# A fused trunk layer on TensorE: the first two products of four projection units are moved between the io projection's second and third product, with 83 working slots instead of 77

## The chip, the cores and the metric

The kernel runs on one core of one Trainium2 chip. The metric is the time of one execution on the device in microseconds (us); lower is better. The kernel before was timed in three runs. One further execution was recorded by the profiler, and all rows of the trace come from that one.

## The reference

The reference computes one layer of a streaming-encoder trunk on a sequence of 2048 rows of width 1024, in fp32:

```python
x_n = rmsnorm(x)
z   = x_n @ W_in          # columns: pool | q | forget | input v | output gate | branch gates
a   = pool_mixer(u)       # trailing means over 2/4/8/16 rows, minus the token, 4 groups of 128
f   = lb + (1 - lb) * sigmoid(zf)
k, q = 1 - f, silu(zq)
S_t = diag(f_t) S_{t-1} + k_t v_t^T          # 4 heads of 128, chunks of 64 rows
o_t = S_t^T q_t ;  o = rmsnorm(o) * silu(zo)
x   = x + (ga * (a @ W_pa) + gb * (o @ W_pb)) @ W_o      # ga, gb = sigmoid(x_n @ W_g + bias)
x   = x + (silu(gate) * val) @ W_down        # val, gate: conv3(rmsnorm(x) @ W_up), d_ff = 2816
out = rmsnorm(x)
```

## The kernel before, in words

**Tiling.** The sequence is cut into four blocks of 512 rows. Two blocks form a pass: the pass `b0 = 0` takes blocks 0 and 1, the pass `b0 = 2` takes blocks 2 and 3, and each runs `mixer` and then `ffn`. Every large product is computed by Strassen-Winograd on 2 x 2 quarters: seven quarter products, P1 to P7, in place of eight, with sums of quarters before and after them. An fp32 operand is split into a high and a low part of type fp32r, and each quarter product is made of three matmuls (high by high, high by low, low by high).

**The forms of x.** Each of the seven products takes its own form of the transposed input (`FORM`): P1 takes B11 and P2 takes B21. Both belong to the pass's first block (in the trace `x_f0h` to `x_f7l`) and are ready before the second block's. P6, P5, P7 and P4 take T2, T1, T3 and T4, sums that contain the second block, and P3 takes B22, the second block itself. The second block is transposed by 32 matmuls of 128 x 128 on TensorE (L646), which write PSUM; VectorE scales and adds them (`x_t`, L703), and each form is then split by a cast on ScalarE (L597) and a subtraction on VectorE (L598).

**The io projection.** `proj_io` (L1105 to L1156) computes v and the output gate z. Its seven products come in the order `IO_ORDER`, P1, P2, P6, P5, P7, P4, P3, and each has 4 x 4 x 3 = 48 matmuls of 128 x 512. P1 leaves `e1` (a copy on ScalarE), P2 gives the first half of v, P6 gives `u2` = e1 - Z (L1133), P7 gives `u3` = Z - e1 (L1135) and the second half of z, P4 the first half of z, and P3 the second half of v. P6, P7 and P4 accumulate in the same four PSUM banks Z, in turn: P4 can overwrite a bank only after `u3` has read it. The product of z with its sigmoid is on GpSimd for one half and on VectorE for the other (L1124).

**The units.** The other columns of W_in are 14 units, listed in `PROJ`: four of kind fq (forget gate and q of a head), two of kind u (the pool branch) and eight of kind g (branch gates). A unit is seven products of 12 matmuls each, in the order `ORDER`, P1, P6, P5, P7, P2, P4, P3. P1 writes the bank X, which ScalarE copies to `e1` (L1018, the names end in `_e`). P2 accumulates onto X, and so must wait for that copy. After P2, a unit's first output is final in X: for fq it is the forget gate (sigmoid at L1189, then L808 on VectorE), for g it is a branch gate (sigmoid at L1234, then a store at L791).

**The weights.** `Stream` holds two planned lists. The raw list is tiles of 256 KB, loaded by SyncE's DMA queue in list order (L182) into `N_RAW = 8` buffers; a buffer is loaded again when its last user has been issued. The operand list is high and low parts, made by a cast on ScalarE (L205) and a subtraction on VectorE (L206) in `N_OPS = 6` buffers. Where a product wants a sum of quarters, the sum is made first, by `plan_io` (L338) for the io projection and by `weights_of_unit` (L397) for a unit, on GpSimd or VectorE. In the pass `b0 = 0` these sums are stored to DRAM (L310), and the pass `b0 = 2` loads them instead of adding again (`sums_of_unit`).

**The order.** The program is written as a loop of products, with side work (forms, the HGRN recurrence, pooling, gates) in tasks that are stepped every 6 matmuls. A list scheduler then sets the order of the instructions of each engine; on the chip each engine takes its list strictly in that order. Working tiles (`e1`, `u2`, gates, q, f) come from a pool of `N_SLOTS = 77` slots of 2112 bytes per partition, and PSUM has 8 banks. When the io projection is over, `prep.append(Task(prepare()))` starts the preparation of later weights by adding DMAs.

Of the kernel before, what the change touches and what calls it, by code (L numbers as in the profile page):

```python
# [49 lines left out]
ORDER = ("P1", "P6", "P5", "P7", "P2", "P4", "P3")  # L50
IO_ORDER = ("P1", "P2", "P6", "P5", "P7", "P4", "P3")
# [5 lines left out]

M_ORDER = (0, 4, 1, 5, 2, 6, 3, 7)

N_SLOTS = 77  # L60
# [18 lines left out]
def tile_trunk(  # L79
# [238 lines left out]
    def plan_io(b0):  # L318
        for p in IO_ORDER:
# [25 lines left out]
    def plan_unit(key, src, kind, i, order, b0):  # L345
        mv, mg = proj_tiles(kind, i)
        if b0:
            unit = sums_of_unit(src, mv, mg, lambda p: lambda: kept["in", (kind, i), SUM_OF[p]])
        else:
            unit = weights_of_unit(src[mv], src[mg], (kind, i))  # L350
        for p in order:
            fn, raws = unit[p]()
            stream.op(key, fn, raws)

    def plan_mixer(b0):
        plan_io(b0)
        for kind, i in PROJ:
            if (kind, i) == ("u", 0):
                plan_one("pw", pool_wt)
            plan_unit("in", w_in_t, kind, i, ORDER, b0)  # L360
# [25 lines left out]
    def weights_of_unit(src_v, src_g, unit):  # L386
# [15 lines left out]
        def plan(p):  # L402
            if p == "P5":
                return (lambda nm: tmp["s1"]), []
            rs = [raw(i) for i in {"P1": (0,), "P2": (1,), "P4": (3,), "P6": (0, 2, 3),
# [700 lines left out]
    def proj_io(b0, forms, late, vd, zd):  # L1106
# [35 lines left out]
        for p in IO_ORDER:  # L1142
# [14 lines left out]

    def mixer(b0, forms, late):
# [5 lines left out]
        proj_io(b0, forms, late, vd, zd)  # L1164
        if b0 == 0:
            prep.append(Task(prepare()))

# [94 lines left out]
        for n, (kind, i) in enumerate(PROJ):  # L1262
            if (kind, i) == ("u", 0):
                held["w"] = stream.get("pw")
            u = Unit(f"{kind[0]}r{b0}_{i}", "in", emits[kind](i))
            for p in ORDER:
                u.multiply(p, forms, late)
                u.after(p)
                if n == len(PROJ) - 1 and p == "P1":
                    mtask = Task(pa_task())  # L1270
# [318 lines left out]
```

## Time and profile before

| what | value |
|---|---|
| median of 3 runs | 2622.06 us (2621.85 to 2622.27) |
| span of the profiled execution | 2614.3 us |
| TensorE busy in it | 2533.7 us (97%) |
| TensorE not busy | 80.6 us |
| VectorE / ScalarE / GpSimd busy | 1967.4 / 1168.9 / 909.3 us |
| mean granted TensorE clock | 0.989 of full speed |

The span runs from the first to the last instruction. The median of the runs is 7.8 us longer, which lies outside the span. A row of the timeline has the start, the time, the engine, the line, the operation with its output and inputs, the count of instructions, and in brackets the idle time just before it and what ended that. The granted clock is the share of full TensorE speed that the chip allowed in a stretch.

### The profile page before, as it was taken

To read this page: it belongs to the slowest core of one execution; us is meant where nothing else is said; L and a number is where in the kernel's file an instruction comes from. 1 tells how busy PE (TensorE), PEld (TensorE's weight loads), DVE (VectorE), ACT (ScalarE), POOL (GpSimd) and SP (SyncE) were. 2 spreads that over 40 slices of the span, in tenths; PEclk is the share of its full clock that TensorE was granted. 3 is DMA by queue.
4 is the path that set the end of the run, shared out by engine and by line. 5 is a ranking of instruction groups with operands and counts; after the bars stand their busy time and mean duration, and the time that the engine had idled before them with its cause. 6 is when DMAs were issued, how large, how long until landed. Compare 5 with 4: busy or idle time off the path is not lost. (4 is left out here: it accounts for less than half of the span.)

```text
span 2614.3 us, 35569 instructions
## 1 busy us (share of the span) xinstructions
PE 2533.7 (97%) x11464; PEld 2064.8 (79%) x11464; DVE 1967.4 (75%) x3390; ACT 1168.9 (45%) x2204; POOL 909.3 (35%) x1253
## 2 busy tenths in 40 slices
PE   7899999989999999999999999999999999999998
PEld 6788888767778888878878788887787888887887
DVE  7898779358799877876476787774778987787845
ACT  5333434224555544555364344442345554445633
POOL 5544343062444343362141111200623433335402
PEclk9999999999999999999999999999999999999999
DMA  6887868888778897587365344346452445545943
GB/s 221 274 213 211 224 189 242 268 275 214 198 188 241 243 240 198 165 305 255 108 195 157 101 135 121 116 145 218 142 173 84 151 150 148 141 141 185 377 142 105
DMA packets 254059, 496.90 MB, mean 190 GB/s; under 512 B 26736, under 2 KB 43248, under 8 KB 253552
## 3 DMA queue, kind: packets, MB, share of 16 engines
q1 hardware_dynamic: 187968, 319.89, 38.9%
q0 software_dynamic: 41504, 110.64, 16.6%
q10 hardware_dynamic: 24400, 64.08, 7.1%
q8 instruction: 91, 1.49, 0.2%
q14 instruction: 96, 0.79, 0.1%
HBM read 384.94 MB, written 187.17 MB: 219 GB/s over the span
## 5 line engine op out<-in xcount | busy, mean ns | idle before, releaser
L205 ACT CAST ops<-raw 128x512 fp32r<-128x512 f32 x732 | 451.6, 620 | 780.1 <-PE dn_P L145 141.1
L206 DVE TENSOR_TENSOR ops<-raw,ops 128x512 fp32r<-128x512 f32 x732 | 564.1, 775 | 214.2 <-ACT ops L205 208.7
L1381 DVE SCALAR_TENSOR_TENSOR e<-h,cols,e 128x512 f32<-128x512 f32 x176 | 142.4, 813 | 29.9 <-ACT e L1379 26.1
L1379 ACT ACTIVATE e<-h,cols 128x512 f32<-128x512 f32 x176 | 142.6, 814 | 24.2 <-DVE h L984 16.9
L1384 DVE SCALAR_TENSOR_TENSOR e<-h,cols,e 128x512 f32<-128x512 f32 x176 | 133.9, 769 | 3.0
L796 POOL DMA_DIRECT2D g_P<-dg_P x154 | 83.7, 545 | 107.6 <-PE dn_P L145 70.0
L1090 POOL TENSOR_TENSOR gf_P<-e,e 128x512 f32<-128x512 f32 x44 | 67.8, 1542 | 153.1 <-DVE e L1390 97.8
L1090 POOL TENSOR_TENSOR gf_P<-gf_P,e 128x512 f32<-128x512 f32 x44 | 60.1, 1366 | 68.5 <-DVE e L1390 68.1
L1374 POOL COPY h<-h 128x2 f32<-128x2 f32 x88 | 40.7, 482 | 113.9 <-DVE h L982 112.0
L1301 POOL TENSOR_TENSOR ya<-ya,gl 128x512 f32<-128x512 f32 x32 | 45.8, 1460 | 98.4 <-issue 49.1
L1376 POOL COPY hist<-h 128x2 f32<-128x2 f32 x88 | 35.3, 401 | 127.3 <-DVE h L984 125.6
L1234 ACT ACTIVATE gt<-gt,cols 128x512 f32<-128x512 f32 x48 | 34.8, 724 | 90.5 <-DVE gt L984 71.1
L1388 ACT ACTIVATE e<-e 128x512 f32<-128x512 f32 x88 | 55.5, 631 | 37.9 <-DVE e L1384 37.4
L984 DVE TENSOR_TENSOR h<-up_u,up_V 128x512 f32<-128x512 f32 x88 | 60.2, 684 | 15.2 <-PE up_V L145 14.8
L1197 POOL TENSOR_TENSOR q<-q,qs 128x512 f32<-128x512 f32 x16 | 22.5, 1407 | 136.0 <-ACT qs L1196 105.0
L846 POOL COPY qm<-q 128x64 f32<-128x64 f32 x64 | 22.4, 367 | 117.0 <-DVE q L852 21.6
L1066 DVE TENSOR_TENSOR x<-x,wo_P 128x512 f32<-128x512 f32 x88 | 56.4, 690 | 6.2 <-PE wo_P L145 6.1
L1066 DVE TENSOR_TENSOR ac<-ac,dn_P 128x512 f32<-128x512 f32 x72 | 46.6, 683 | 13.4 <-PE dn_P L145 13.3
L1404 POOL DMA_DIRECT2D dg_P<-gf_P x88 | 52.5, 596 | 10.9 <-POOL gf_P L1090 6.5
L1450 POOL TENSOR_TENSOR fss<-fss 128x1 f32<-128x1 f32 x16 | 4.6, 289 | 141.5 <-ACT fj L1439 141.5
L619 POOL TENSOR_SCALAR ro<-so 128x4 f32<-128x4 f32 x16 | 5.2, 323 | 135.6 <-ACT sq L956 135.4
L1018 ACT COPY up_e<-up_X 128x512 f32<-128x512 f32 x44 | 25.8, 586 | 56.7 <-PE up_X L145 51.6
(1265 smaller groups left out, 8332.4 us busy)
## 6 DMA issues: line engine op xcount, KB each, us to landing
g_P<-dg_P POOLq DMA_DIRECT2D x154, 256.0 KB, 6.2
raw<-in_w_up_t SPq DMA_DIRECT2D x132, 256.0 KB, 3.3
raw<-in_w_in_t SPq DMA_DIRECT2D x98, 256.0 KB, 3.3
dg_P<-gf_P POOLq DMA_DIRECT2D x88, 256.0 KB, 3.9
raw<-in_w_io SPq DMA_DIRECT2D x68, 256.0 KB, 4.9
dg_P<-e SPq DMA_DIRECT2D x66, 256.0 KB, 3.3
raw<-in_w_dn SPq DMA_DIRECT2D x66, 256.0 KB, 3.0
x<-in_x SPq DMA_DIRECT2D x64, 256.0 KB, 5.3
```

Source lines behind the costliest of these rows:

```text
L205: self.mark = act.copy(hi, v)
L206: dve.tensor_tensor(lo, v, f32(hi), ALU.subtract)
L796: eng.dma_start(t, d)
L984: dve.tensor_tensor(dst, t, ps, ALU.add if how == "add" else ALU.subtract)
L1066: dve.tensor_tensor(t, t, ps[j], ALU.add if sg > 0 else ALU.subtract)
L1090: pin(pool.tensor_tensor(t, x0, x1, op))
L1301: pool.tensor_tensor(y[m, hf], y[m, hf], g, ALU.add)
L1379: in_turn(act.activation(t, h[:, 2:], AF.Identity, bias=col(o_cb + mt), scale=col(o_cw + 4 * MF + mt)))
L1381: in_turn(second(dve.scalar_tensor_tensor(t, h[:, 1 : 1 + TB], col(o_cw + 2 * MF + mt), t, ALU.mult, ALU.add)))
L1384: dve.scalar_tensor_tensor(t, h[:, 0:TB], col(o_cw + mt), t, ALU.mult, ALU.add)
L1388: in_turn(act.activation(g, g, AF.Silu))
L1404: pool.dma_start(d, t)
```

## The change

The four units of `IN_HEADS`, that is fq 0, g 0, g 1 and fq 1, have their P1 and P2 taken out of their own place and put between the second and the third product of the io projection: 8 products of 12 matmuls, in each of the two passes. Their other five products stay at the unit's place in `PROJ`, in the old order. A new function, `in_sequence`, lists all products in that order, and the planned weight list and the mixer's loop both follow it. In the pass `b0 = 0` these early products load their raw quarters by themselves (`own`), so that the quarters 0 and 1 of these four units are loaded twice: 8 more loads of 256 KB. The preparation still begins after the io projection's last product. The pool has 83 slots instead of 77, which takes 6 x 2112 = 12,672 bytes more per partition, and `dynamic_dma_scratch_size=4096` is passed where nothing was passed before.

```diff
+IN_HEADS = (("fq", 0), ("g", 0), ("g", 1), ("fq", 1))
+
+def in_sequence():
+    seq = [("io", p) for p in IO_ORDER[:2]]
+    seq += [(u, p) for u in IN_HEADS for p in ("P1", "P2")]
+    seq += [("io", p) for p in IO_ORDER[2:]]
+    for u in PROJ:
+        if u == ("u", 0):
+            seq.append(("pw", None))
+        seq += [(u, p) for p in ORDER if u not in IN_HEADS or p not in ("P1", "P2")]
+    return seq
...
-N_SLOTS = 77
+N_SLOTS = 83
...
-    def plan_io(b0):
-        for p in IO_ORDER:
+    def plan_io(b0, p):
+        if True:
...
+        for u, p in in_sequence():
+            if u == "io":
+                plan_io(b0, p)
+            elif u == "pw":
                 plan_one("pw", pool_wt)
...
+                fn, raws = units[u][p]()
+                stream.op("in", fn, raws)
...
-        def raw(i):
+        def raw(i, own):
+            if own:
+                return stream.raw(src[i])
...
+            own = head and p in ("P1", "P2")
+            rs = [raw(i, own) for i in {"P1": (0,), "P2": (1,), "P4": (3,), "P6": (0, 2, 3),
...
+        for what, p in in_sequence():
...
+            if what == "io":
+                run_io(p)
+                if b0 == 0 and p == IO_ORDER[-1]:
+                    prep.append(Task(prepare()))
+                continue
...
+            u.multiply(p, forms, late)
+            u.after(p)
...
-    nc = bacc.Bacc("TRN2", target_bir_lowering=False, num_devices=1)
+    nc = bacc.Bacc("TRN2", target_bir_lowering=False, num_devices=1, dynamic_dma_scratch_size=4096)
```

In the changed kernel a line of the old kernel stands 14 to 18 lines lower: L145 becomes L159, L646 becomes L664, L206 becomes L220, L1018 becomes L1036 and L1234 becomes L1251. The number at the end of a name is an allocation number and means nothing.

The first place is TensorE's list in the pass `b0 = 0`, behind the last transpose of the second block. Before, io P6 (`io0_Z`, on T2) stands right behind it:

```order
L646 MATMUL x1_t7_629<-ident_79,x1_xs2_1_331 128x128
L646 MATMUL x1_t7_629<-ident_79,x1_xs3_1_342 128x128
L145 MATMUL io0_Z_0_701<-ops8_477,x1_T20h_537 128x512 x2
L145 MATMUL io0_Z_0_701<-ops8_477,x1_T20l_538 128x512
L145 MATMUL io0_Z_0_701<-ops9_510,x1_T21h_565 128x512 x2
```

Now the unit fq 0 (`fr0_0`) begins there, and further down the last rows of g 0's P2, then g 1's P2, then io P6 follow directly on each other (`gr0_0` and `gr0_1` are the banks X of g 0 and g 1):

```order
L664 MATMUL x1_t7_600<-ident_79,x1_xs3_1_342 128x128
L159 MATMUL fr0_0_X_662<-x0_f0h_232,ops8_472 128x512
...
L159 MATMUL gr0_0_X_719<-x0_f7l_275,ops11_632 128x512
L159 MATMUL gr0_0_X_719<-x0_f7h_274,ops11_632 128x512
L159 MATMUL gr0_1_X_766<-x0_f4h_256,ops13_695 128x512
...
L159 MATMUL gr0_1_X_766<-x0_f7h_274,ops13_695 128x512
L159 MATMUL io0_Z_0_893<-ops16_778,x1_T20h_518 128x512
```

The 32 transposes still stand in one piece ahead of the first unit, and 84 unit matmuls come between them and io P6; the last 12 (P2 of fq 1) stand in the middle of io P6.

The second place is ScalarE's list at the same point, where the units' copies (`e1`), sigmoids and casts were put in. Before, only casts stood there:

```order
L205 CAST ops11_667<-w11s1_664 128x512
L597 CAST x1_T11h_758<-x1_t11_559 128x512
L205 CAST ops12_715<-w12s0_712 128x512
L205 CAST ops13_745<-w13s0_742 128x512
L205 CAST ops14_779<-w14s0_776 128x512
L597 CAST x1_T12h_829<-x1_t12_608 128x512
```

Now:

```order
L1206 ACT_TABLE_LOAD
L1206 ACTIVATE f0_0_717<-fr0_0_X_662 128x512
L1036 COPY gr0_0_e1_743<-gr0_0_X_719 128x512
L1251 ACTIVATE gt0_0_0_762<-gr0_0_X_719,cols_84 128x512
L809 DMA gd0_0_0_764<-gt0_0_0_762 128x512
L615 CAST x1_T12h_787<-x1_t12_579 128x512
L1036 COPY gr0_1_e1_797<-gr0_1_X_766 128x512
L219 CAST ops16_778<-w16s1_775 128x512
L219 CAST ops17_811<-w17s1_808 128x512
L1251 ACTIVATE gt0_0_1_826<-gr0_1_X_766,cols_84 128x512
```

The copy `gr0_1_e1` stands behind the gate `gt0_0_0`, which reads the bank of g 0 after its P2. So g 1's P2, right behind g 0's P2 on TensorE, has to wait for a copy that is behind a sigmoid of g 0's P2.

The third place is VectorE's list ahead of `u3`, which reads the banks Z after io P7 and before io P4. Before:

```order
L206 TENSOR_TENSOR ops23_1055<-raw39_879,ops23_1055 128x512
L598 TENSOR_TENSOR x1_B222l_1005<-x1_b2_606,x1_B222h_1004 128x512
L598 TENSOR_TENSOR x1_T43l_1017<-x1_t43_1014,x1_T43h_1016 128x512
L598 TENSOR_TENSOR x1_B223l_1021<-x1_b3_634,x1_B223h_1020 128x512
L1135 TENSOR_TENSOR io0_u3_0_1044<-io0_Z_0_701,io0_e1_0_434 128x512
L984 TENSOR_TENSOR z0_1_0_1046<-io0_u3_0_1044,io0_V_0_837 128x512
```

Now:

```order
L616 TENSOR_TENSOR x1_B223l_1077<-x1_b3_605,x1_B223h_1076 128x512
L220 TENSOR_TENSOR ops25_1090<-w25s0_1087,ops25_1090 128x512
L220 TENSOR_TENSOR ops26_1113<-w26s0_1110,ops26_1113 128x512
L220 TENSOR_TENSOR ops27_1136<-w27s0_1133,ops27_1136 128x512
L220 TENSOR_TENSOR ops28_1156<-raw44_1050,ops28_1156 128x512
...
L220 TENSOR_TENSOR ops31_1215<-raw47_1095,ops31_1215 128x512
L1153 TENSOR_TENSOR io0_u3_0_1204<-io0_Z_0_893,io0_e1_0_434 128x512
L1002 TENSOR_TENSOR z0_1_0_1206<-io0_u3_0_1204,io0_V_0_1033 128x512
```

The splits of the second block (T4, B22) no longer stand directly ahead of `u3`; operands of P7 and P4 do. Counted from the program's start, 10 more VectorE instructions and 96 more matmuls stand ahead of `u3` than before.

More of the change, by code (lines that the diff above doesn't have):

```diff
@@ L1140, in after, with run @@
                 out_v(1, j, (u2[j], "sub"))
-        for p in IO_ORDER:
+        def run(p):
             xs = need(forms, FORM[p], late)
@@ L1163, in mixer @@
         md, od, gd = {}, {}, {}
-        proj_io(b0, forms, late, vd, zd)
-        if b0 == 0:
-            prep.append(Task(prepare()))
+        run_io = proj_io(b0, forms, late, vd, zd)
         queue = []
```

43 lines of the change are left out of this document (20 added, 23 removed).

## The prediction

> **What bounds the kernel now.** I read the page first, then TensorE's waits, then the windows and the timeline at the places that the change touches.
>
> ```profile
> span 2614.3 us, 35569 instructions
> PE 2533.7 (97%) x11464; PEld 2064.8 (79%) x11464; DVE 1967.4 (75%) x3390; ACT 1168.9 (45%) x2204; POOL 909.3 (35%) x1253
> ```
>
> TensorE (PE) is busy for 97% of the span; 80.6 us are left. The matmuls stay the same in number, so the change can win only idle time of TensorE and time at a low clock. TensorE's waits (total us, times, longest) say what is idle:
>
> ```profile
> PE pa L145 <- ACT mxs_2h L597: 5.8, 1, 5.8
> PE io_Z L145 <- DVE io_u L1135: 4.1, 1, 4.1
> PE x_t L646 <- DVE x_t L703: 3.0, 2, 1.5
> ```
>
> The largest are one by one, and two of these three rows belong to the first pass of the io projection. The windows over that stage (length, busy time of PE, PEld, DVE, ACT, POOL, then granted clock, DMA share, GB/s) show it:
>
> ```profile
> 44.00:54.10 10.10, 7.11 (x24) 5.60 (x23) 9.84 (x16) 4.02 (x8) 3.12 (x6) 0.50 0.16 53
> 54.10:88.20 34.10, 31.71 (x137) 25.40 (x135) 34.02 (x43) 18.04 (x31) 16.79 (x12) 1.00 0.77 269
> 88.20:95.10 6.90, 5.18 (x13) 4.12 (x14) 6.76 (x11) 2.44 (x4) 3.73 (x3) 0.51 0.27 97
> ```
>
> VectorE works through 34.02 of 34.10 us: a backlog. Around it lie two stretches at half clock (0.50, 0.51), each behind idle time of TensorE. The timeline shows the places:
>
> ```profile
> 50.59 1.22 PE L145 MATMUL io_Z<-ops,x_T20h 128*128 128x512 f32 x2 [1.53 <-DVE x_t L703]
> ...
> 89.92 1.19 PE L145 MATMUL io_Z<-ops,x_T40h 128*128 128x512 f32 x2 [4.10 <-DVE io_u L1135]
> ...
> 95.09 0.62 PE L145 MATMUL io_Z<-ops,x_T40h 128*128 128x512 f32 x2
> 97.87 0.63 PE L145 MATMUL io_Z<-ops,x_T40h 128*128 128x512 f32 x2
> ```
>
> Twelve matmuls took 95.09 - 89.92 = 5.17 us at half clock and 97.87 - 95.09 = 2.78 us at full clock: 0.232 us a matmul, and 2.39 us lost per twelve slow ones.
>
> **The change part by part.**
>
> *The wait of P4.* VectorE reaches `u3` late:
>
> ```profile
> 88.49 0.68 DVE L598 TENSOR_TENSOR x_B223l<-x_b,x_B223h 128x512 fp32r<-128x512 f32 x1
> 89.09 0.68 DVE L1135 TENSOR_TENSOR io_u<-io_Z,io_e 128x512 f32<-128x512 f32 x1
> ```
>
> P7 had ended 4.10 us before 89.92, at about 85.8, so VectorE was some 3.3 us behind. After, 96 matmuls more stand ahead of P7's end, 96 x 0.232 = 22.3 us, and 10 VectorE instructions more, 10 x 0.68 = 6.8 us. That leaves 15.5 us to make up 3.3 us, so the backlog is gone. The 4.10 us go down to the normal `u3`, and the half clock behind it goes too: -4.1 - 2.4 = **-6.5 us**. If VectorE's f (which waits for a sigmoid) or a late operand holds the queue, some 2 us of it could come back.
>
> *The start.* The transposes still stand ahead of everything, with their two waits of 1.5 us on `x_t`. Behind them fq 0's P1 needs only a free bank and first-block data, no `x_t`. Of the 1.53 us at 50.59 some remains, since ScalarE and VectorE empty the banks of the transposes first. The additions and operands of io P6 no longer stand among the evacuations, but six operands of the units do. I take **-0.8 us**, half of that wait. The range runs from +1.5 (operands in the way for as long as the present wait) to -3: the 1.53 us, and a clock that comes back with some six matmuls fewer at half rate, 6 x 0.2 = 1.2 us.
>
> *A new wait.* g 1's P2 now follows g 0's P2 directly, and on ScalarE the copy that it needs stands behind g 0's sigmoid, a DMA issue and a cast. Queued behind that are the casts of io P6's first operands, and TensorE waits for the copy. Such rows of the trace are:
>
> ```profile
> 118.80 0.59 ACT L1018 COPY fr_e<-fr_X 128x512 f32<-128x512 f32 x1 [2.27 <-PE fr_X L145]
> 119.28 0.62 ACT L205 CAST ops<-raw 128x512 fp32r<-128x512 f32 x1
> 150.77 0.67 ACT L1234 ACTIVATE gt<-gr_X,cols 128x512 f32<-128x512 f32 x1
> ...
> 1447.23 1.13 PE L895 MATMUL pl<-q,k 128*128 128x128 f32 x8 [1.21 <-DVE q L820]
> 1450.00 0.77 PE L145 MATMUL gr_X<-x_f4h,ops 128*128 128x512 f32 x1 [1.64 <-ACT gr_e L1018]
> 1453.52 0.40 PE L145 MATMUL gr_X<-x_f6h,ops 128*128 128x512 f32 x1
> ```
>
> Sigmoid, cast and copy are 0.67 + 0.62 + 0.59 = 1.88 us; with the end of the last matmul I take **+2.1 us** (1.3 without the cast, 2.6 if ScalarE is late). At 1450 the same kind of wait, 1.64 us and 1.21 us shortly before it, brought the half clock: eight matmuls took 3.52 us in place of 1.86, so 1.7 us lost. Here I count half of that chance: **+0.85 us**.
>
> [...]
>
> *io P3's operands.* GpSimd makes them in pairs of additions, behind its products of z:
>
> ```profile
> 91.30 5.62 POOL L1124 TENSOR_TENSOR z<-z,zs 128x512 f32<-128x512 f32 x4 [9.90 <-ACT zs L1123]
> 96.89 3.11 POOL L338 TENSOR_TENSOR w24s<-w24s,raw 128x512 f32<-128x512 f32 x2
> ...
> 107.21 3.40 POOL L338 TENSOR_TENSOR w27s<-w27s,raw 128x512 f32<-128x512 f32 x2 [0.63 <-DMA raw<-in_w_in_t]
> ...
> 103.47 1.32 PE L145 MATMUL io_V<-ops,x_B220h 128*128 128x512 f32 x5
> 114.26 0.51 PE L145 MATMUL io_V<-ops,x_B223h 128*128 128x512 f32 x1 [0.85 <-DVE ops L206]
> 121.26 0.50 PE L145 MATMUL fr_Z<-x_T20h,ops 128*128 128x512 f32 x1 [1.62 <-DVE ops L206]
> ```
>
> Two additions take 3.0 to 3.4 us, TensorE's use of one operand 2.8 us. The first pair ended at 100.0, 3.5 us ahead of its use at 103.47. With `u3` prompt, z starts about 3.3 us earlier, but P4 ends 6.5 us earlier; the cover shrinks by 3.2 us, to nothing, with an operand's cast and subtraction still to come. I take **+1.5 us** (0 to +3.5). The wait at 121.26, on a unit's operand made behind that chain, becomes shorter, since two products of fq 0 no longer ask for operands there: **-1.0 us** (0 to -1.6).
>
> *The branch stage.* The 5.83 us on `mxs_2h` come from a fetch:
>
> ```profile
> 474.81 2.24 SPq L182 DMA_DIRECT2D raw<-in_w_pb_t  x2
> 477.14 1.44 SPq L796 DMA_DIRECT2D mx<-md  x2
> ...
> 486.57 0.80 PE L145 MATMUL pa<-mxs_2h,ops 128*128 128x512 f32 x1 [5.83 <-ACT mxs_2h L597]
> ```
>
> In SyncE's new list the fetch stands ahead of the raw loads that stood ahead of it, so it can be issued about 2.3 us earlier, the two loads' own time: **-2.0 us** (0 to -5, where the half clock behind it goes as well).
>
> *Costed at nothing.* The 8 more loads (2 MB) fall into 44 to 54 us, where the DMA share is 0.16 against 0.77 later, and cost nothing unless they hold io P6's raw tiles; that cover gone, a load is late by its time to landing, 3.3 us by the page. In the second pass no operand is summed, and the moved products replace each other: 0, from -3 to +4, for the waits at 1447 and 1450 lie there and will be dealt anew. More slots cannot cost time on their own (0 to -1). [...]
>
> ```profile
> g_P<-dg_P POOLq DMA_DIRECT2D x154, 256.0 KB, 6.2
> raw<-in_w_in_t SPq DMA_DIRECT2D x98, 256.0 KB, 3.3
> ```
>
> No wait of TensorE names g_P, so I take 0; one transfer late by its own time is the upper end, +6.2 us. [...]
>
> **The sum.** -6.5 - 0.8 + 2.1 + 0.85 + 1.5 - 1.0 - 2.0 = -5.85 us on the profiled 2614.3, so 2608.5. The median lies 7.8 us above the span; it goes from 2622.06 to about **2616**, with a range of its own from 2611 to 2621: the widest open terms, -3 to +4 in the second pass and some 2 us each at start, new wait, P3 and fetch, seldom fall to one side together.
>
> **The rivals.**
>
> *The wins all come (2608).* The start gives 3.0, the new wait costs 1.3 with no half clock, P3 waits no longer than now, and the fetch brings 5: -6.5 - 3.0 + 1.3 - 1.0 - 5.0 = -14.2. For it: the present loss is all there in rows. Against it: a new order seldom loses no wait elsewhere.
>
> *The new waits eat it (2622).* The wait at g 1's P2 costs 2.1 + 1.7, P3 3.5, and neither start nor fetch moves: -6.5 + 3.8 + 3.5 - 1.0 = -0.2. For it: 1450 shows that very wait with its half clock. Against it: that wait had another just ahead of it.
>
> *VectorE becomes the bound of the units behind the io projection (2628).* This is the slower side.
>
> ```profile
> 122.00:200.00 78.00, 76.28 (x373) 63.43 (x373) 62.86 (x149) 25.15 (x52) 30.56 (x36) 1.00 0.85 231
> 141.00:161.00 20.00, 18.28 (x96) 15.28 (x96) 19.85 (x43) 7.78 (x19) 7.39 (x10) 1.00 0.75 256
> L206 DVE TENSOR_TENSOR ops<-raw,ops 128x512 fp32r<-128x512 f32 x12 | 10.6, 900 | 0.0
> ```
>
> Five units of 84 matmuls take 97.5 us now, and VectorE 62.86 / 78 x 97.5 = 78.6 us of work. After, four of them lose 24 matmuls each, 22.3 us, so TensorE needs 75.2 us. VectorE loses 8 operand subtractions of 0.68 (the like at 88.49), 5.4 us, and needs 73.2, or 97%. In this stage such subtractions took a mean of 0.90 us, by the last row, so a denser order can lengthen its work. At 10% more it needs 80.5: 5.3 us of waits, and, spread over four waits with a half clock of 1.7 each as at 1450, 12.1 us. -5.85 + 12.1 = +6.2. It decides from the point at which VectorE's work is over 75.2 us. For it: 19.85 of 20 us busy at 141 to 161, where TensorE loses 1.72. Against it: over the 78 us VectorE has 15.1 us free, and the recurrence's work can slide.
>
> *That the change doesn't do what it says* can be left out: the order shows the products where they should be.
>
> **How the numbers follow.** My forecast has 0.48, the large win 0.16, the waits that eat it 0.20, VectorE's bound 0.16. A measurement of this kernel can tell about 0.2%, 5.2 us, from no change. The forecast's -6 lies close to that bound: 0.58 of its chance is beyond it and 0.42 within. Faster: 0.48 x 0.58 + 0.16 = 0.44. Same: 0.48 x 0.42 + 0.20 x 0.85 + 0.16 x 0.10 = 0.39. Slower: the rest, 0.17. The range runs from the large win's 2608, less 1, to VectorE's 2628, plus 1: 2607 to 2629.
>
> **What would show it.** Right: no wait of `io_Z` on `io_u` over 1 us in the first pass and no half clock behind it; a wait of `gr_X` on `gr_e` of about 2 us near 70 us; waits of `io_V` on operands of 1 to 3 us; the wait of `pa` near 480 at 3 to 4 us. Wrong: `io_u` still late; VectorE over 97% busy from the end of io P3 over five units, with TensorE waiting for `ops` or `q` there; GpSimd's transfers (g_P) later than 6.2 us with waits of TensorE or VectorE on them in the last stage; or a change of over 5 us outside the first 130 us and the branch stage.

## The result and the profile after

The changed kernel takes 2656.64 us (median of 4 runs, 2654.20 to 2658.75), the kernel before 2621.95 us (4 runs, 2621.22 to 2622.27) on the same chip. The ratio is 1.0134, with a 95% interval of 1.0120 to 1.0148: 34.7 us slower. The prediction was 2616 us, with a range up to 2629.

The head of the page after:

```profile
span 2656.9 us, 35557 instructions
PE 2548.5 (96%) x11464; PEld 2070.6 (78%) x11464; DVE 1970.1 (74%) x3390; ACT 1166.5 (44%) x2204; POOL 905.4 (34%) x1253
```

The instruction counts of the engines are those of before. The busy time of VectorE, ScalarE and GpSimd moved by under 4 us each. TensorE's idle time rose from 80.6 to 2656.9 - 2548.5 = 108.4 us, and the same 11464 matmuls took 14.8 us longer. The mean granted clock tells of that. The row of the cores view after:

```profile
core 0: 2656.9 us, clock 0.983
```

It was 0.989 before. Every clock record in the traces of before and after is 1.00 or 0.50, so 2 x 0.011 x 2614.3 = 58 us at half clock became 2 x 0.017 x 2656.9 = 90 us. The loss in the spans is 27.8 us of waits and 14.8 us of clock, 42.6 us. That is more than the 34.7 us of the medians, because the first profile of before was of an execution below that kernel's median, and that of after 2 us above its own. A run's time lies only some 2 us above its span (2658.75 and 2656.9 us here, 2615.40 and 2613.6 in `e7`), so the span of 2614.3 belongs to some 2616 us. The 7.8 us in the table of before are thus not time outside the span: some 6 of them are the distance of that execution from the median.

TensorE's waits after (the releasing tile behind the arrow; total us, times, longest):

```profile
PE pl L913 <- DVE q L838: 14.5, 4, 5.1
...
PE io_Z L159 <- DVE io_u L1151: 5.9, 1, 5.9
```

One wait of `io_Z` on `io_u` is left, and it isn't the one of before. The timeline of TensorE after shows where these waits stand, in order of time:

```profile
50.11 0.80 PE L159 MATMUL fr_X<-x_f0h,ops 128*128 128x512 f32 x1 [1.28 <-DVE x_t L721]
71.59 0.50 PE L159 MATMUL gr_X<-x_f4h,ops 128*128 128x512 f32 x1 [2.34 <-ACT gr_e L1036]
102.75 0.51 PE L159 MATMUL io_Z<-ops,x_T30h 128*128 128x512 f32 x1 [0.42 <-DVE ops L220]
106.86 0.50 PE L159 MATMUL io_Z<-ops,x_T31h 128*128 128x512 f32 x1 [1.06 <-DVE ops L220]
134.44 0.50 PE L159 MATMUL io_V<-ops,x_B222h 128*128 128x512 f32 x1 [1.54 <-DVE ops L220]
138.14 0.50 PE L159 MATMUL io_V<-ops,x_B223h 128*128 128x512 f32 x1 [0.64 <-DVE ops L220]
144.53 0.79 PE L159 MATMUL fr_Z<-x_T20h,ops 128*128 128x512 f32 x1 [3.34 <-DVE ops L220]
173.67 2.05 PE L913 MATMUL pl<-q,k 128*128 128x128 f32 x8 [4.75 <-DVE q L838]
220.65 0.47 PE L159 MATMUL fr_Z<-x_T30h,ops 128*128 128x512 f32 x1 [2.57 <-DVE fr_u L1038]
245.50 0.49 PE L800 MATMUL pm<-pl_1h,ops 128*128 128x512 f32 x1 [4.09 <-ACT pl_1h L615]
514.60 0.79 PE L159 MATMUL pa<-mxs_3h,ops 128*128 128x512 f32 x1 [5.96 <-ACT mxs_3h L615]
1442.41 1.19 PE L159 MATMUL io_Z<-ops,x_T30h 128*128 128x512 f32 x2 [5.91 <-DVE io_u L1151]
1503.66 3.75 PE L913 MATMUL pl<-q,k 128*128 128x128 f32 x16 [3.05 <-DVE q L838]
```

The first seven rows are the io stage and the first unit behind it. The wait at the io projection's P4 (4.10 us, with a half clock) is gone, and the rows at 50, 71, 134 and 138 us are those that were forecast. The two near 105, where P7's operands (on T3) come late, were not. From 144 us on the rows are new, or longer than before. One of them is longer by less than the first profile of before says: `fr_Z` waited 1.62 us there and 2.72 us in `e7`, a second execution of the same kernel.

The best view of where the time went is a comparison at equal work: the start of the matmul that has the same amount of matmul work ahead of it (in us at full clock), after less before, worked out from the two timelines of TensorE. In the changed kernel the io projection's P4 ends ahead of 100, its P3 at 108, the five units behind it near 200; the first pass ends near 1300 in all.

| kernel: us later than the first profile of before | at 100 | 140 | 200 | 300 | 1320 | 1400 | end |
|---|---|---|---|---|---|---|---|
| after | -4.0 | 12.7 | 22.7 | 23.8 | 26.4 | 38.3 | 43.5 |
| first products early in the first pass alone | -3.1 | 12.5 | 20.6 | 22.1 | 23.5 | 24.5 | 26.8 |
| the same, sums on VectorE | -2.9 | 9.6 | 10.3 | 11.2 | 12.5 | 12.3 | 11.4 |
| after, sums on VectorE | -5.3 | 7.4 | 7.9 | 9.2 | 13.5 | 18.2 | 22.1 |
| g 3 to g 6 early, first pass, sums on VectorE | -4.0 | -1.5 | -3.1 | -3.2 | 3.4 | 3.1 | 2.3 |
| early in the second pass alone | 6.7 | 11.1 | 10.2 | 14.5 | 13.3 | 23.9 | 28.5 |
| g 3 to g 6 early, second pass, early splits | 6.8 | 11.3 | 9.7 | 14.2 | 17.9 | 16.2 | 16.4 |
| before with 83 slots | 4.8 | 8.5 | 7.7 | 11.9 | 13.6 | 14.8 | 14.8 |
| before with 81 slots | 4.7 | 9.9 | 8.0 | 10.8 | 10.7 | 9.2 | 10.3 |
| before with 78 slots | 4.4 | 4.5 | 3.5 | 8.2 | 3.8 | 3.4 | 2.4 |
| before again | 1.0 | 1.0 | 1.0 | 0.6 | 0.4 | -1.0 | -0.8 |

After is 4.0 us ahead behind P4, level when the io projection ends (0.2 at 108), 22.7 us behind when the next five units are done, and loses 17 us more from 1320 on, in the second pass. Two executions of before stay within 1 us of each other all along. Yet `e13` below, which differs from before in the DMA scratch alone, is 3 to 5 us behind all along and costs no time by its median, so a difference of that size between two rows shows nothing; a step within one row says more.

### The profile page after: what moved, and what is told of

The parts are those of the page before. It is cut to its first block, busy times and chain, and to the rows that moved or that the text cites. A ratio compares the mean times of both kernels' runs of the same rounds, so it can differ in the third digit from the quotient of the medians.

```text
span 2656.9 us, 35557 instructions
## 1 busy us (share of the span) xinstructions
PE 2548.5 (96%) x11464; PEld 2070.6 (78%) x11464; DVE 1970.1 (74%) x3390; ACT 1166.5 (44%) x2204; POOL 905.4 (34%) x1253
## 3 DMA queue, kind: packets, MB, share of 16 engines
q0 software_dynamic: 41504, 110.64, 16.2%
## 4 chain that ended last, share of the span: by engine, by line
PE 67%; DVE 3%; issue 1%; ACT 1%; DMA 0%; POOL 0%; DVEq 0%; POOLq 0%; ACTq 0%; SPq 0%
PE dn_P L159 15%; PE up_Z L159 13%; PE up_V L159 9%; PE up_X L159 8%; PE gr_Z L159 2%; PE wo_P L159 2%; PE pa L159 2%; PE gr_V L159 2%; PE pb L159 2%; PE gr_X L159 2%; PE io_Z L159 1%; PE fr_Z L159 1%; DVE ops L220 1%; PE fr_X L159 1%; PE fr_V L159 1%
## 5 line engine op out<-in xcount | busy, mean ns | idle before, releaser
L220 DVE TENSOR_TENSOR ops<-raw,ops 128x512 fp32r<-128x512 f32 x732 | 565.4, 776 | 233.6 <-ACT ops L219 223.4
L1407 DVE SCALAR_TENSOR_TENSOR e<-h,cols,e 128x512 f32<-128x512 f32 x176 | 141.9, 810 | 30.8 <-ACT e L1405 26.4
L1405 ACT ACTIVATE e<-h,cols 128x512 f32<-128x512 f32 x176 | 142.5, 814 | 23.9 <-DVE h L1002 18.0
L1002 DVE TENSOR_TENSOR h<-up_u,up_V 128x512 f32<-128x512 f32 x88 | 60.1, 683 | 13.8 <-PE up_V L159 13.3
L1251 ACT ACTIVATE gt<-gt,cols 128x512 f32<-128x512 f32 x48 | 34.9, 728 | 68.3 <-DVE gt L1002 48.3
L913 PE MATMUL pl<-q,k 128*128 128x128 f32 x256 | 38.9, 305 | 17.2 <-DVE q L838 14.5
```

Source lines behind the costliest of these rows:

```text
L220: dve.tensor_tensor(lo, v, f32(hi), ALU.subtract)
L1002: dve.tensor_tensor(dst, t, ps, ALU.add if how == "add" else ALU.subtract)
L1405: in_turn(act.activation(t, h[:, 2:], AF.Identity, bias=col(o_cb + mt), scale=col(o_cw + 4 * MF + mt)))
L1407: in_turn(second(dve.scalar_tensor_tensor(t, h[:, 1 : 1 + TB], col(o_cw + 2 * MF + mt), t, ALU.mult, ALU.add)))
```

## The experiments

The theory that the experiments came to, step by step: the moved products are two of the three in a unit whose operands need no sum (P4 is the third), so they were cover, that is matmul work during which GpSimd's additions and VectorE's operands for the other five were made. Units of five products ask for the sums faster than they come (first pass), and in the second pass, where no sum is made, the splits of the second block's tiles come late in lists that are worked through in order. The rivals are in the expectations: the slots or the scratch, the forget gates with their sigmoid among the moved units, or the moved products wherever they stand.

### Slots, first pass, second pass

`e1_slots_only` is the kernel before with 83 slots and the scratch of 4096, in the old order. `e2_first_pass` and `e3_second_pass` are the changed kernel with the early products in one pass only:

```diff
+def in_sequence(b0):
+    heads = IN_HEADS if b0 == 0 else ()    # e2; e3: if b0 > 0
+    seq += [(u, p) for u in heads for p in ("P1", "P2")]
+        seq += [(u, p) for p in ORDER if u not in heads or p not in ("P1", "P2")]
```

> The kernel before with 83 slots and the smaller DMA scratch, in the old order of products. Theory A (the new order costs the time): no change, 2622 us within 4 us. Rival C (slots or scratch cost it): a good part of the 35 us is here, 2635 us or more, with GpSimd's transfers landing late.

> The changed kernel with the early products in the pass b0 = 0 alone. Aligned by matmuls done, the trace after is 26 us behind when the first pass ends and 16 to 17 us further behind in the second. Theory A: about 2622 + 26 = 2648 us. If the loss of the second pass is only a shadow of a later start, all of it comes with this one: 2656 us. Rival C: 2635 to 2645, the rest being there without any early product.

> The changed kernel with the early products in the pass b0 = 2 alone. Theory A: about 2622 + 16 = 2638 us, with the 5.9 us wait of io_Z on io_u there and 3 to 5 us of waits of pl on q. If the weights' additions (first pass only) are what makes units short of products slow, this one costs little: 2622 to 2628 us.

Measured: `e1` 2626.44 us, 1.0022 [1.0012, 1.0032] of before; `e2` 2643.05, 1.0089 [1.0074, 1.0104]; `e3` 2642.23, 1.0086 [1.0071, 1.0101]. Over `e1`, by the medians, the first pass costs 16.6 us and the second 15.8. With the 5.8 us of the slots (by the ratio) that is 38 us, against 34.7. So both passes lose, neither loss is the shadow of the other, and the slots lose too, which had been costed at nothing.

### Which units are early

```diff
-IN_HEADS = (("fq", 0), ("g", 0), ("g", 1), ("fq", 1))
+IN_HEADS = (("g", 0), ("g", 1), ("g", 2), ("g", 3))    # e4
+IN_HEADS = (("g", 4), ("g", 5), ("g", 6), ("g", 7))    # e5
+IN_HEADS = (("g", 6), ("g", 7))                        # e6
+IN_HEADS = (("g", 3), ("g", 4), ("g", 5), ("g", 6))    # e9
```

> The changed kernel with the four early units being g 0 to g 3, no fq among them. Theory B (the forget gates of the early fq units block VectorE's list, which waits for their sigmoids while splits pile up, and the recurrence starts against a late VectorE): most of the loss goes, 2615 to 2630 us, and VectorE no longer idles for 3 to 7 us in the middle of the io projection. Rival D (any unit that lost its P1 and P2 runs out of operands or of cover): the loss stays, 2645 us or more.

> The changed kernel with g 4 to g 7 as the early units: the io stage has the same eight early products, but the units right behind it, where the recurrence begins, keep all seven products. Theory E (the time goes where units of five products leave the recurrence, the pooling and the operands too little matmul work as cover): the first pass is as fast as with slots alone or up to 9 us faster, since io gains; only the second pass's wait on u2 (some 12 us) stays: 2625 to 2636 us. Rival F (the sigmoids and copies inside the io stage, and the splits queued behind them, cost it, whichever units are early): as with g 0 to g 3, about 2650 us.

> Only g 6 and g 7 early: four early products, 48 matmuls. Both their sigmoids stand earlier in io P6, and half as many slots are held. Theory F for the second pass (the last early sigmoid holds ScalarE's list, the splits of T3, T4 and B22 pile up behind it and u2 comes 6 us late): with half the early products the pile-up is smaller, the wait on u2 is under 2 us, and the whole is near the slots-only kernel, 2622 to 2628 us. Rival: the wait comes from the slots and stays, 2635 us.

> The changed kernel with g 3 to g 6 as the early units. With g 7 among them the task that prepares the branch stage began in the io stage and put casts of the pooled output far too early into ScalarE's list; that spoilt the two kernels with g 7, and here it cannot happen. Theory E (units of five products lose their cover or run short of operands wherever they stand): in the first pass no loss at fq 0, and 5 us or more at each short unit, some 20 us in all behind 330 us; 2645 to 2655 us. Rival G (only the units beside the first heads of the recurrence suffer): the first pass is no slower than with slots alone, only the second pass's loss of 12 to 14 us is left, about 2636 us.

`e4`: 2650.68 us, 1.0118 [1.0103, 1.0133]. That the forget gates alone do the harm is out: the sigmoids of four ordinary gates hold the lists in the same way. In the first pass, with two short units (g 0 and g 1) among the five behind the io projection and not four, it is level with before at 108 and some 10 us behind at 200. The second pass of `e4`, ScalarE and TensorE in one timeline:

```profile
1423.98 0.69 ACT L1251 ACTIVATE gt<-gr_X,cols 128x512 f32<-128x512 f32 x1 [6.94 <-PE gr_X L159]
...
1434.99 1.19 PE L159 MATMUL io_Z<-ops,x_T30h 128*128 128x512 f32 x2 [6.01 <-DVE io_u L1151]
```

ScalarE stands 6.94 us at a gate's sigmoid, and 11 us later the io projection waits 6.01 us, as in the changed kernel.

`e5` (2666.70 us, 1.0172 [1.0157, 1.0187]) and `e6` (2653.41, 1.0125 [1.0110, 1.0140]) tell nothing of the question they were made for. The task of the branch product is created when P1 of g 7 is done. With g 7 early, that is in the io stage, and the casts of the pooled output stand in ScalarE's and VectorE's lists long before their data is there. The timeline of `e6`:

```profile
421.12 0.62 ACT L615 CAST mxs_2h<-mx 128x512 fp32r<-128x512 f32 x1 [12.14 <-DMA mx<-md]
421.77 0.69 DVE L616 TENSOR_TENSOR mxs_2l<-mx,mxs_2h 128x512 fp32r<-128x512 f32 x1 [11.11 <-ACT mxs_2h L615]
423.12 0.80 PE L159 MATMUL fr_Z<-x_T40h,ops 128*128 128x512 f32 x1 [7.19 <-DVE fr_u L1042]
```

One fetch that is late holds ScalarE for 12.14 us, VectorE behind it for 11.11 and TensorE for 7.19.

`e9`: 2646.06 us, 1.0093 [1.0078, 1.0108]. Now the units right behind the io projection keep their seven products. There it loses less (6.5 us behind at 200, not 22.7), and it falls from 6.5 to 24.8 us behind between 200 and 400, where the short units now stand. The loss follows the short units, that is those left with five products.

### Who makes the sums

GpSimd makes the sums s1 to s4 of the units' operands. In `e8_sums_dve` VectorE does, in the changed kernel; in `e12_first_sums_dve` in `e2`; in `e10_before_sums_dve` in the kernel before.

```diff
-            pool.tensor_tensor(t, x0, x1, ALU.add)
+            dve.tensor_tensor(t, x0, x1, ALU.add)
```

> The changed kernel with the units' weight sums added by VectorE instead of GpSimd (0.7 us instead of 1.3 to 1.7 each). Theory D (in the first pass, operands made by GpSimd come too late for units of five products): the waits on operands behind io go, 8 to 15 us faster than the changed kernel, 2640 to 2648 us. Rival E (the recurrence's and the gates' chains between the engines are short of cover): no gain, or slower, since VectorE gets more work, 2655 to 2665 us.

> The early products in the first pass alone, and the units' sums added by VectorE. The trace with both passes changed and these sums was 7 us behind the first profile at the end of the first pass, where slots alone were 13 behind. If the passes add up: 2619 to 2624 us, 20 us faster than with GpSimd's sums (2643). If the sums gain as much in the old order, it is slower than the kernel before with the same sums.

> The kernel before with the units' weight sums added by VectorE instead of GpSimd, nothing else. In the changed kernel this edit won 16 us. Theory D (short units wait for GpSimd's additions): a unit of seven products has time for them, so at most 5 us are won here, 2615 to 2622 us. Rival: the additions on GpSimd cost the same in any order, and about 15 us are won here too, 2605 us.

`e8`: 2640.53 us, 1.0080 [1.0063, 1.0097]; by the ratios 14 us better than the changed kernel. `e12`: 2625.92, 1.0014 [1.0005, 1.0024], 20 us better than `e2`. `e10`: 2617.22, 0.9986 [0.9976, 0.9995], 3.5 us better than before. The same edit is worth 14 to 20 us with short units and 3.5 us with long ones, although it puts more work on VectorE. It doesn't take the whole loss away: with VectorE's sums in both, `e12` is still 0.28% or 7 us slower than `e10`, the 83 slots included. The table shows which part is left. From 100 to 140 `e2` loses 15.6 us and `e12` 12.5; from 140 to 200 `e2` loses 8.1 and `e12` 0.7. The windows over the end of the io projection and the units behind it, first of the changed kernel, then of `e8` (length, busy time of PE, PEld, DVE, ACT, POOL, then granted clock, DMA share, GB/s):

```profile
100.00:260.00 160.00, 137.84 (x622) 111.81 (x622) 127.05 (x236) 48.12 (x98) 75.38 (x70) 0.94 0.72 214
```

```profile
100.00:260.00 160.00, 148.39 (x690) 120.33 (x689) 135.62 (x292) 56.45 (x120) 45.45 (x52) 0.97 0.79 235
```

In the changed kernel VectorE is busy for 127 of 160 us and TensorE gets through 622 matmuls. With 56 VectorE instructions more in the same time it gets through 690. So VectorE was not full; it was late. What makes it late shows at the wait of 4.75 us at 173.67. VectorE and GpSimd of the changed kernel just ahead of it, in the timeline:

```profile
168.24 1.55 DVE L826 TENSOR_SCALAR f<-f,lbt 128x512 f32<-128x512 f32 x1
169.70 1.75 DVE L220 TENSOR_TENSOR ops<-w45s,ops 128x512 fp32r<-128x512 f32 x1
171.37 1.48 DVE L935 TENSOR_TENSOR f<-f 128x256 f32<-128x256 f32 x1
172.78 0.41 DVE L827 TENSOR_SCALAR k<-f 128x512 f32<-128x512 f32 x1
173.11 0.41 DVE L838 TENSOR_TENSOR q<-q,f 128x256 f32<-128x256 f32 x1
...
168.20 1.30 POOL L414 TENSOR_TENSOR w48s<-raw,raw 128x512 f32<-128x512 f32 x1
169.58 1.32 POOL L414 TENSOR_TENSOR w48s<-w48s,raw 128x512 f32<-128x512 f32 x1
170.86 1.70 POOL L414 TENSOR_TENSOR w50s<-raw,raw 128x512 f32<-128x512 f32 x1
```

Three VectorE instructions took 1.55, 1.75 and 1.48 us, beside one GpSimd addition each. Alone they take 0.55 (the same line at 1432.14, below), 0.68 (a subtraction of that shape, in the prediction's row at 88.49) and 0.41 (one of that shape, at 173.11). The `q` that TensorE waits for came 3.1 us late by that; in `e8` the same wait is 1.87 us (at 167.48) and not 4.75. The additions beside it are those of later operands: work ahead of its need, beside work that is needed.

The wait of `fr_Z` at 144.53 is of another kind. GpSimd, ScalarE and VectorE ahead of it, in the timeline:

```profile
137.61 1.61 POOL L414 TENSOR_TENSOR w36s<-w36s,raw 128x512 f32<-128x512 f32 x1
139.25 1.14 ACT L219 CAST ops<-w36s 128x512 fp32r<-128x512 f32 x2 [1.61 <-POOL w36s L414]
138.00 3.48 DVE L1142 TENSOR_TENSOR z<-z,zs 128x512 f32<-128x512 f32 x2
143.80 2.36 DVE L220 TENSOR_TENSOR ops<-w36s,ops 128x512 fp32r<-128x512 f32 x2
```

The sum was ready at 139.2 us and its casts at 140.4, but VectorE came to the subtraction only at 143.80, since it was still at z and v of the io projection. Additions beside it took part in that (two products of z in 3.48 us, which take 0.68 us each alone, from 1467.00 us on). But with VectorE's sums and a short fq 0 the wait is as long (0.98 + 2.24 us in `e8`), and with GpSimd's sums and a whole fq 0 it is 2.7 us (`e7`, `e9`); only with VectorE's sums and a whole fq 0 is it gone (`e15` below). So either is enough for it: the additions, or the lack of fq 0's P1, 12 matmuls or 2.8 us of work ahead of P6.

### The second pass

The changed kernel's second pass makes no sums. Its wait of 5.91 us at 1442 comes from the lists. VectorE there, in the timeline:

```profile
1432.14 0.55 DVE L826 TENSOR_SCALAR f<-f,lbt 128x512 f32<-128x512 f32 x1 [6.84 <-ACT f L1206]
1432.65 0.69 DVE L616 TENSOR_TENSOR x_T30l<-x_t,x_T30h 128x512 fp32r<-128x512 f32 x1
...
1441.59 0.67 DVE L1151 TENSOR_TENSOR io_u<-io_e,io_Z 128x512 f32<-128x512 f32 x1
```

VectorE stands 6.84 us at the f of the last early unit, which waits for its sigmoid, and then works for 9 us through the splits and operands that stand between it and `io_u`. `e11_second_early_splits` is `e3` with the splits of T1 spaced closer, so that those of T3 and T4 come ahead of the sigmoid. `e14_second_g36_splits` has that too, with g 3 to g 6 as the early units.

```diff
-            yield 5
+            yield 1 if src == ("x", 3) else 5
```

> The early products in the second pass alone, as before, but with the splits of T1 of that pass issued every matmul step in place of every fifth, so that the splits of T3, T4 and B22 stand ahead of the early gates' sigmoids in ScalarE's list. Theory F (splits pile up behind the last sigmoid, u2 comes late): the wait of io_Z on io_u of 6 us and its half clock go, 8 to 12 us faster than the kernel it is made from (2642), 2630 to 2634 us. Rival: u2 is late for VectorE's load or for slots; no gain, 2640 us or more.

> The second pass alone with g 3 to g 6 as the early units, and the early splits of T1. Theory: the second pass has two losses, the pile-up behind the last sigmoid (taken away here) and the first heads of the recurrence, whose short units fq 0 to fq 1 no longer cover its waits (they are whole here). Then next to nothing is left over slots alone: 2625 to 2630 us, against 2642 with fq 0 to fq 1. If the early products themselves cost it (slots, banks, copies in the io stage): 2635 us or more.

`e11`: 2640.90 us, 1.0075 [1.0060, 1.0090], no clear difference from `e3`, where 8 to 12 us had been expected. `e14`: 2632.63, 1.0048 [1.0034, 1.0062], 7 us better than `e11`. TensorE in the second pass of `e11`:

```profile
1423.48 0.73 PE L160 MATMUL io_V<-ops,x_T10h 128*128 128x512 f32 x2 [0.69 <-ACT f L1207]
1481.07 1.13 PE L914 MATMUL pl<-q,k 128*128 128x128 f32 x8 [1.71 <-DVE q L839]
1485.25 3.75 PE L914 MATMUL pl<-q,k 128*128 128x128 f32 x16 [3.05 <-DVE q L839]
```

and of `e14`:

```profile
1423.25 0.74 PE L160 MATMUL io_V<-ops,x_T10h 128*128 128x512 f32 x2 [0.78 <-ACT gt L1252]
1485.93 1.13 PE L914 MATMUL pl<-q,k 128*128 128x128 f32 x8 [1.24 <-DVE q L839]
1488.70 0.50 PE L160 MATMUL gr_X<-x_f4h,ops 128*128 128x512 f32 x1 [1.65 <-ACT gr_e L1037]
```

In both the wait for `io_u` is gone. `e11` keeps the waits for `q` of the first head, since its units fq 0, g 0, g 1 and fq 1 are still short; `e14` has the waits that before has. In the table above `e14` loses nothing from 1320 on (17.9 to 16.4), `e3` loses 15 us there and `e11` 9.5. Its median is still 6 us above that of `e1`. That rest isn't in the second pass of its profile, and it stays open; the runs of `e1` range from 2621.74 to 2631.37, and its profile is of the slowest.

### The slots

`e13_scratch_only` is the kernel before with the scratch of 4096 alone; `e17_81_slots` and `e18_78_slots` have 81 and 78 slots besides.

> The kernel before with the smaller DMA scratch alone; every engine's list is the same as before, word for word. 83 slots and the scratch together cost 5.8 us (0.12 to 0.32%). [...] If the slots do it, through the order that the scheduler finds with them: no change, 2620 us within 3.

> The kernel before with 81 slots (and the scratch of 4096). The order of its instructions differs from before just as with 83 slots (from the pooling matmuls of the first pass on), but the table load ahead of the sigmoid of z waits, as with 77 slots, for an old transfer and not for z. Theory table load (the 6 us come from the 1.28 us load that stands behind z with 83 slots): the load runs before z, the io projection takes as long as before, and the time is within 0.1% of before, 2618 to 2623. Theory order (the later order costs the 6 us): 2625 to 2628, as with 83 slots.

> The kernel before with 78 slots (and the scratch of 4096): one slot more than before, an order nearer to that of before than with 83, but the table load ahead of the sigmoid of z waits for z. Theory table load: 4 to 8 us slower than before, 2624 to 2628, with the loss between 90 and 130 us and waits of TensorE on operands there. Theory order: at most 2 us from before.

`e13`: 2619.94 us, 0.9998 [0.9988, 1.0007]: the scratch costs nothing. `e17`: 2627.24, 1.0027 [1.0017, 1.0037]. `e18`: 2617.75, 0.9997 [0.9988, 1.0006]. The theory of the table load fell: it stood behind z with 78 slots, which cost nothing, and ahead of z with 81, which cost 7 us. The theory of the later order fell as well, though both times are as it said, since the profile of `e17` has its whole loss ahead of that order (9.9 us behind at 140, 10.3 at the end). At equal work, the 81 and 83 slots of `e17`, `e1`, `e3`, `e11` and `e14` lose 3.2 to 4.6 us in one step, between 110 and 115 us of work. The 77 and 78 of before, its repetition, `e10`, `e13` and `e18` lose 0.4 us at most there. That place is the first wait of `pl` for `q`. The timeline of `e13`, three engines:

```profile
144.66 2.43 DVE L206 TENSOR_TENSOR ops<-raw,ops 128x512 fp32r<-128x512 f32 x2
147.01 0.42 DVE L809 TENSOR_SCALAR k<-f 128x512 f32<-128x512 f32 x1
...
149.30 2.08 POOL L397 TENSOR_TENSOR w44s<-raw,raw 128x512 f32<-128x512 f32 x1 [3.37 <-DVE q L822]
...
147.90 1.13 PE L895 MATMUL pl<-q,k 128*128 128x128 f32 x8 [1.71 <-DVE q L820]
```

and of `e17`:

```profile
146.03 3.48 DVE L206 TENSOR_TENSOR ops<-raw,ops 128x512 fp32r<-128x512 f32 x2
149.44 1.51 DVE L809 TENSOR_SCALAR k<-f 128x512 f32<-128x512 f32 x1
...
147.26 1.71 POOL L397 TENSOR_TENSOR w44s<-raw,raw 128x512 f32<-128x512 f32 x1
149.04 1.63 POOL L397 TENSOR_TENSOR w44s<-w44s,raw 128x512 f32<-128x512 f32 x1
...
151.44 1.13 PE L895 MATMUL pl<-q,k 128*128 128x128 f32 x8 [3.89 <-DVE q L820]
```

The lists of TensorE, VectorE and GpSimd are the same in the two up to there. With 77 slots GpSimd stands still for 3.37 us before `w44s`, and VectorE's work on `k` and `q` runs alone. With 81 slots `w44s` starts at once, VectorE's three instructions take 4.99 us and not 2.85, and TensorE waits 3.89 us and not 1.71, with a half clock behind it. The wait for a slot had kept GpSimd out of VectorE's way. This is the first-pass mechanism again, in an order of instructions that nobody changed.

### All repairs together

`e15_first_g36_dve`: g 3 to g 6 early in the first pass alone, with the sums on VectorE. `e16_both_g36_repaired`: the changed kernel with g 3 to g 6, the sums on VectorE and the splits as in `e11`. `e7_before_again` is the kernel before.

> The first pass alone with g 3 to g 6 early and the units' sums on VectorE. With the sums on GpSimd the trace lost 16 us at these four short units (from 280 to 400 us of work). Theory D (short units wait for operands that GpSimd adds, or for a VectorE that is slowed by it): these 16 us are gone, 2620 to 2626 us. If short units suffer from lost cover for other reasons: still 10 us lost there, 2632 us or more.

> All repairs together: g 3 to g 6 early in both passes, sums on VectorE, early splits of T1 in the second pass. If the losses found are all there are, it is where slots alone with these sums would be: 2620 to 2626 us, over 30 us faster than the changed kernel and no faster than the kernel before with these sums (2617). If the io stage's gain of 4 us a pass comes through: 2612 to 2616 us.

> The kernel before, unchanged, profiled again on this chip. Its times say what one kernel scatters by from run to run. If the first profile (span 2614.3, 7.8 below its median) was a usual one, the span is again about 7 below the time; if it was a lucky execution, the span lies within 3 us of the time and the waits behind io P3 are longer than in the first profile.

`e15`: 2618.87 us, 0.9995 [0.9986, 1.0004]. `e16`: 2621.20, 1.0004 [0.9995, 1.0013]. `e7`: 2615.40, one run, span 2613.6. With all repairs the loss of 35 us is gone, and there is no difference from before that can be measured. `e16` is 3.5 us ahead at 100, as the changed kernel is, and level at 140. The only kernel that beats before is `e10`, which moves no product at all.

## Why the prediction was wrong, point by point

- *P4's wait, -6.5:* right. The wait and the half clock behind it are gone.
- *The start, -0.8:* the wait at 50.11 is 1.28 us in place of 1.53. Right in its direction, a quarter of a microsecond in size.
- *The new wait at g 1's P2, +2.1, and half of a half clock, +0.85:* right, 2.34 us. The half clock came whole; its windows are below.
- *io P3's operands, +1.5:* 1.54 + 0.64 in place of 0.85, so +1.3 by the waits' rows; at equal work 4.2 us went between 100 and 108. P7's operands waited too, 0.42 + 1.06, which had not been foreseen.
- The first four terms sum to -4.35, and after is 4.0 us ahead behind P4. The places hold up to there, but that the two sums agree is partly luck: P7's 1.48 us and the other half of the half clock (0.85) are in no term, and before has had its waits of 0.85 and 1.62 us by that amount of work.
- *The wait of `fr_Z`, -1.0: this is the step that failed first.* The prediction said that it "becomes shorter, since two products of fq 0 no longer ask for operands there". It was 3.34 us, with a half clock, against 1.62 (2.72 in `e7`). This gain is the only term that the sum has for the five units behind the io projection, and they lost 22.5 us (from 0.2 at 108 to 22.7 at 200). The products were counted as load on the engines that make operands, and they were their cover: the two that moved away ask for operands that need no sum, and the five that stay ask for four sums in 5 x 12 x 0.232 = 13.9 us of matmuls, not 19.5.
- *VectorE as the bound of the units (2628, a chance of 0.16):* the place was right, the mechanism wrong. The rival asked whether VectorE's work exceeds TensorE's time; by the windows it was busy for 127 of 160 us. What decided was when an instruction ran and what ran beside it. The five units cost 22.5 us, against 12.1 in the rival. Of these, 12.5 us are lost by 140 us of work, at the waits of `fr_Z` (3.34 us) and of `pl` (1.73 on an operand's cast, then 4.75 on `q`) and the half clocks behind both. `e8`, `e12` and `e15` show two parts of the cause: GpSimd's additions, which are most of what is lost after 140, and the short units themselves, which lose before 140 also with the sums on VectorE. How much of the first part is additions that come late for their own operands, and how much is VectorE held up by them, was not separated, except at the waits for `q` shown, where it was VectorE held up.
- *The second pass, "0, from -3 to +4": the second step that failed.* It was 15.8 us. The term rested on there being no sums, which is true, and on the waits at 1447 and 1450. It left out that an instruction that waits for an early product holds everything that stands behind it in its engine's list (6.84 us at f, then 9 us of splits and operands), and that the first head's `q` lost its cover as well. `e4`, `e11` and `e14` show both.
- *Slots, "cannot cost time on their own (0 to -1)": the third.* They cost 6 us in the old order (`e1`), 3.2 to 4.6 of it at one wait. In the changed order their share isn't known. The scratch cost nothing (`e13`: 2619.94 us, and GpSimd's transfers of `g_P` landed after a median of 6.1 us, 6.2 before); no run shows that it reaches those transfers.
- *The branch stage, -2.0:* 5.96 in place of 5.83 us, no gain. On SyncE's queue only one of the two fetches moved ahead of a raw load (501.22 us); the other, of the tile that TensorE waits for, went out at 504.68, behind the raw load of 504.25, and ScalarE stood idle for 7.24 us until it landed.
- *The median 7.8 us above the span:* this was some 2 us and the scatter between executions. It made the forecast neither better nor worse in sign.
- *The rows of TensorE's waits:* the three rows shown there aren't the three largest (`x_t` waits 9.0 us for `x_xs` in all, `wo_P` 6.3 us for `x`). That changes no term.

What had been named as the sign of an error, "a change of over 5 us outside the first 130 us and the branch stage", is what the profile shows.

## What to carry to other kernels

Before a piece of work is moved out of a stage to cover a wait, ask what it covered where it stood, and count the operands that the rest of that stage needs per microsecond without it. In lists that are worked through in order, look up what stands behind each instruction that the moved work releases (6.84 us at f and 9 us of work behind it, in the changed kernel's second pass). An earlier start of work that nobody waits for yet (a free slot, an addition ahead of its need) can cost time, when it runs beside the instruction that is waited for (4.99 us for three instructions in `e17`, 2.85 in `e13`). Move it to the engine that is waited for (14 us won in `e8`, 20 in `e12`), or keep it where it was held back (as in `e13`, whose wait was 1.71 us and not 3.89).

## What the runs showed of the hardware

**VectorE beside GpSimd.** Instructions of VectorE whose inputs all lie in SBUF took 2.8 and 3.6 times as long beside a GpSimd addition: `f<-f,lbt` 1.55 us at 168.24 and 0.55 at 1432.14, `k<-f` 1.51 us in `e17` and 0.42 in `e13`. Each of the two reads a single 128x512 tile. Instructions with an input in PSUM weren't lengthened where this was looked at: in the changed kernel the 28 of L1002 (such as `v<-io_u,io_V`) that ran beside a GpSimd `TENSOR_TENSOR` for 0.3 us or more took 0.67 to 0.69 us, like the others of that line. The lengthened `k<-f` ended at 150.95 us, 0.28 us behind the GpSimd addition that ended at 150.67, and the three at 168.24, 169.70 and 171.37 ended 0.29, 0.55 and 0.29 us behind theirs.

**The clock.** Half clock came behind a wait of TensorE of 2.34 us. The windows of the changed kernel around it:

```profile
68.60:72.00 3.40, 1.06 (x5) 0.56 (x4) 0.69 (x1) 2.25 (x4) 1.26 (x1) 1.00 0.59 216
72.00:75.40 3.40, 3.40 (x10) 2.64 (x9) 2.59 (x4) 0.67 (x2) 0.00 (x0) 0.50 0.22 62
```

TensorE worked for 1.06 of the 3.40 us before the clock fell to 0.50, and the clock stayed there for 3.4 us. In the clock records of the traces of before and after, every stretch between two changes lasted a whole number of 3.41 us. Worked out from these records and the matmuls, with the full-clock stretches cut into windows of 3.41 us, the clock fell behind 24 windows, with at most 1.67 us of TensorE's work in each, and stayed full behind 1468, with at least 1.52 us in each. In these traces, what a wait cost depended on how it lay across these windows. The same wait of `fr_Z`, 2.72 us in `e13` and 2.73 us in `e17`, was spread over two windows in `e13`, and the clock stayed full:

```profile
119.45:122.86 3.41, 2.47 (x11) 1.68 (x9) 3.41 (x5) 2.70 (x5) 2.19 (x2) 1.00 0.77 197
122.86:126.27 3.41, 1.63 (x7) 1.37 (x8) 3.41 (x6) 0.00 (x0) 0.71 (x1) 1.00 0.95 318
```

In `e17` it fell into one, and half clock followed from 125.20 us on:

```profile
121.78:125.20 3.42, 0.75 (x3) 0.66 (x4) 3.42 (x7) 0.68 (x2) 0.00 (x0) 1.00 1.03 375
```

At half clock the changed kernel ran for one to three such windows at a time (3.41, 6.83 or 10.24 us in its clock records). With the clock at 0.50 a window of matmuls loses half of its 3.41 us, an estimate of 1.7 us. The 33 us more of half clock in the changed kernel are over a third of its loss in the spans (14.8 of 42.6 us).
